# Attention of a two-block model: the steps written out in one fixed order

## Chip, cores, metric

The kernel runs on one core of a Trainium2 chip. The metric is the device time of one execution in microseconds, as a median of runs.

## What is computed

The model is two blocks on 512 tokens of width 1024, all in float32. The first block has two layers with feed-forward parts and a pooling or convolution mixer. The second has a gated linear attention (GLA) and a softmax attention side by side, gates for both, a merge and a feed-forward part. The change is in the softmax attention of the second block:

```python
qx = apply_rope(rms_norm_2(split_heads(aq, N_Q_HEADS, HEAD_DIM), q_norm), cos, sin)   # 8 heads of 128
kx = apply_rope(rms_norm_2(split_heads(ak, N_KV_HEADS, HEAD_DIM), k_norm), cos, sin)  # 2 heads, 512 tokens
kc = rms_norm_2(split_heads(ak_c, N_KV_HEADS, HEAD_DIM), k_norm)                      # 256 context tokens
s = jnp.einsum('bqhgd,bkhd->bhgqk', q_blk, k) * (HEAD_DIM ** -0.5)                    # k: 512 + 256 rows
p = jax.nn.softmax(s, axis=-1)
o = jnp.einsum('bhgqk,bkhd->bqhgd', p, v)
```

The merge then takes sigmoid(gate_a) * (attn @ w_br_attn) + sigmoid(gate_g) * (gla @ w_br_gla). The 16 gate projections (8 row tiles for each of the two gates) don't depend on the attention.

## The kernel before

Everything is kept transposed: a tile has 128 channels as partitions and 512 tokens as columns. Each float32 operand is split in a high and a low part of the type fp32r (`split`, L181: ScalarE casts the high part, VectorE subtracts it for the low part), and each product is three matmuls (`mm3`, L191: low weight, high weight, and high weight with the low part of the moving operand). A projection (`proj`, L197) is eight such products over 512 columns: 24 matmuls. Weights come by DMA from SyncE's queue into three raw buffers and are split into two buffers for high and two for low parts (`weights` of block 2, L578; `chunk`, L172).

The program's text is not the order in which the engines run. A scheduler with a timeline of its own orders each engine's instructions ahead of time by their place in the text and by when their inputs are ready in that timeline. On the chip each engine then takes them in that order. `keep_in_program_order` (L188) holds an instruction at its place. In the GLA phase just ahead, `run` (L697) goes through a list of steps and pins the first matmul of each step; the GLA steps and half projections (`halves`, L749; `gate_steps`, L797) alternate there. The last six steps of that phase already include gate projections.

The attention phase (L1009) has no pins but in small helpers. Its text: query 0; the two key heads, each for the 256 context and the 512 own tokens (squares, token sums on TensorE, a power on GpSimd in `rstd`, the sums spread by TensorE, the rotation `rotate` L1106, and a split); the values of six token tiles; and then for each of eight heads the query of the next head (L1060), a gate projection (L1066), and two halves of 256 query rows. A half has two tiles of scores (L1078 to L1080, 6 matmuls of 384 columns each), the softmax (L1081 to L1086), 12 transposes of the probabilities in three groups (L1094), the split of each group into PTh and PTl, and 18 matmuls for the product with values (L1099). There are two probability buffers (`probs`). PSUM has one pj bank for projections, one po bank, two tp banks and two sc buffers of two banks (L587). The query's token sums take the pj bank (L1023). `merge_gates(3)` (L1103) makes the last three gates. Each gate is stored to DRAM and read back by the merge.

The rope table (L1014) is loaded into memory that the last gate of the GLA phase used, so its DMA waits for that gate's DMA.

Of the kernel before, what the change touches and what calls it, by code (L numbers as in the profile page):

```python
# [9 lines left out]
F32 = mybir.dt.float32  # L10
# [21 lines left out]
GH = 4  # L32
# [116 lines left out]
class Builder:  # L149
# [35 lines left out]
    def pin(self, ins):  # L185

        if self.mark:
            self.tc.keep_in_program_order(ins)  # L188
            self.mark = False

    def mm3(self, ps, whi, wlo, xhi, xlo, start, stop):  # L191
        mm = self.nc.tensor.matmul
        self.pin(mm(ps, wlo, xhi, start=start, stop=False))  # L193
        mm(ps, whi, xhi, start=False, stop=False)  # L194
        mm(ps, whi, xlo, start=False, stop=stop)  # L195
# [501 lines left out]
    def run(self, steps):  # L697

        for step in steps:
            self.mark = True  # L700
            step()
        self.mark = False
# [83 lines left out]

    def merge_gates(self, n):
        for i in range(self.ngates, min(self.ngates + n, 2 * KT)):
            w = self.wm(self.gate_at(i))
            ps = self.psum("pj")  # L790
            self.proj(ps, w, self.hs)
            sg = self.ptmp.tile([P, T], F32, name="sg", tag="sq")
            self.sigmoid(sg, ps)
            self.nc.scalar.dma_start(self.gsave[i], sg)
            self.ngates = i + 1
# [180 lines left out]
    def value_rows(self, ps, wv, tt, ks, per, width):  # L976
        for k in ks:
# [6 lines left out]
            self.pin(mm(o, xl[:, t0:t0 + P], hi[:, s], start=(k == 0), stop=False))  # L984
            mm(o, xh[:, t0:t0 + P], hi[:, s], start=False, stop=False)  # L985
            mm(o, xh[:, t0:t0 + P], lo[:, s], start=False, stop=(k == KT - 1))  # L986
# [22 lines left out]
    def attention_phase(self, ctx):  # L1009
# [7 lines left out]
        def query(hd):  # L1017
            w = self.wm(WM_AQ + hd)
            ps = self.psum("pj")
            self.proj(ps, w, self.hs)  # L1020
            sq = self.ptmp.tile([P, T], F32, name="qsq", tag="sq")
            nc.scalar.activation(sq, ps, AF.Square)
            sums = self.psum("pj", "qsum")  # L1023
            self.token_sums(sums, sq, 4)
            r = self.rstd(sums[:, 0:4], 4, P, "q")
            rs = self.psmall.tile([P, 4], F32, name="rs4")
            nc.vector.tensor_scalar(rs, r[:, 0:4], QSCALE, None, ALU.mult)
            qf = p2.tile([P, T], F32, name="qf", tag="qf")
            nc.scalar.activation(qf, ps, AF.Copy, scale=self.vec("q_norm_2", 0, 1))
            qr = self.rotate(p2, qf)  # L1030
# [26 lines left out]
        for hd in range(8):  # L1057
            kv = hd // 4
            qh, ql, rs = nxt
            if hd < 7:  # L1060
                nxt = query(hd + 1)
# [185 lines left out]
```

## Time and profile before

| | |
|---|---|
| median of 3 runs | 2756.4 us (2752.97 to 2758.74) |
| the profiled execution | 2755.51 us, its span 2753.7 us |
| TensorE busy | 2701.2 us, 98% of the span |
| VectorE, ScalarE busy | 56%, 35% of the span |
| mean granted clock of TensorE | 0.997 |
| attention phase, first query projection to first branch product | 2032.2 to 2265.3 us |

A wait is time in which an engine stands still before an instruction; the profile names what ended it. A busy TensorE is not yet one at full speed: the granted clock of a stretch says which share of 2.4 GHz it had, and 0.5 is 1.2 GHz.

### The profile page before, as it was taken

The numbers are of one execution on the slowest core, as the hardware profiler recorded it, in microseconds if no ns is written. First come the engines' busy times: TensorE is split into PE (matmuls) and PEld (weight loads), VectorE is DVE, ScalarE is ACT, GpSimd is POOL, SyncE is SP. The second block draws the span as 40 slices with busy tenths as digits, with TensorE's granted clock in tenths as the row PEclk, the third lists the DMA queues.
The fourth block names the chain that finished last, engine by engine and source line by source line (L and its number), as shares of the span: only waits on it lengthen the run. The fifth ranks groups of instructions, "written<-read, shape, count | busy, mean of one in ns | idle before, by whom it ended". The sixth has DMA issues, their size and how long they took to land.

```text
span 2753.7 us, 34613 instructions
## 1 busy us (share of the span) xinstructions
PE 2701.2 (98%) x14005; PEld 2329.1 (85%) x14005; DVE 1532.4 (56%) x2499; ACT 950.6 (35%) x1474; POOL 36.0 (1%) x47
## 2 busy tenths in 40 slices
PE   7999999999999999999999998999999999999999
PEld 6888889888898888888988888888888888988887
DVE  6645567444466455754774556555546665554433
ACT  4222244222242222322432234544356662333322
POOL 0000000000000000000000000000010000000000
PEclk9999999999999999999999999999999999999999
DMA  8745543444536454433364542211111125333332
GB/s 316 253 140 189 184 146 122 147 133 135 166 116 209 140 173 156 128 101 99 118 213 142 169 139 78 73 54 47 58 62 62 58 78 183 96 100 94 98 99 78
DMA packets 102978, 354.42 MB, mean 129 GB/s; under 512 B 11425, under 2 KB 11681, under 8 KB 102689
## 3 DMA queue, kind: packets, MB, share of 16 engines
q1 hardware_dynamic: 100512, 348.00, 39.2%
q10 hardware_dynamic: 2304, 4.20, 0.4%
q8 instruction: 110, 1.80, 0.3%
q14 instruction: 52, 0.42, 0.0%
HBM read 343.76 MB, written 8.39 MB: 128 GB/s over the span
## 4 chain that ended last, share of the span: by engine, by line
PE 95%; DVE 2%; ACT 2%; DMA 1%; issue 0%; POOL 0%; SPq 0%; DVEq 0%; ACTq 0%
PE mm L193 29%; PE mm L194 28%; PE mm L195 28%; PE mm L984 1%; PE mm L986 1%; PE mm L985 1%; PE mm L904 1%; PE mm L991 1%; PE mm L1094 1%; ACT whi L182 1%; PE mm L446 0%; PE mm L492 0%; PE nR L273 0%; PE sc L1078 0%; DVE wlo L183 0%
## 5 line engine op out<-in xcount | busy, mean ns | idle before, releaser
L193 PE MATMUL mm<-hh,wlo 128*128 128x512 f32 (+1 forms) x2344 | 883.6, 379 | 2.8 <-ACT hh L289 1.8
L194 PE MATMUL mm<-hh,whi 128*128 128x512 f32 (+1 forms) x2344 | 878.2, 377 | 0.0
L195 PE MATMUL mm<-hl,whi 128*128 128x512 f32 (+1 forms) x2344 | 869.1, 377 | 0.4 <-DVE hl L290 0.3
L182 ACT CAST whi<-wraw 128x1024 fp32r<-128x1024 f32 (+1 forms) x443 | 456.8, 1034 | 907.1 <-PE mm L195 481.7
L183 DVE TENSOR_TENSOR wlo<-wraw,whi 128x1024 fp32r<-128x1024 f32 (+1 forms) x443 | 532.6, 1204 | 292.3 <-ACT whi L182 290.7
L193 PEld LDWEIGHTS mm<-hh,wlo 128*128 128x128 f32 x2344 | 442.4, 189 | 81.8 <-ACT hh L289 2.2
L194 PEld LDWEIGHTS mm<-hh,whi 128*128 128x128 f32 x2344 | 441.9, 189 | 77.5
L195 PEld LDWEIGHTS mm<-hl,whi 128*128 128x128 f32 x2344 | 437.0, 189 | 80.6 <-DVE hl L290 0.8
L194 PE MATMUL mm<-g,whi 128*128 128x512 f32 (+1 forms) x1147 | 416.1, 363 | 0.0
L193 PE MATMUL mm<-g,wlo 128*128 128x512 f32 (+1 forms) x1147 | 416.0, 363 | 0.0
L195 PE MATMUL mm<-g,whi 128*128 128x512 f32 (+1 forms) x1147 | 413.7, 362 | 0.0
L312 DVE SCALAR_TENSOR_TENSOR x<-mm,mod,x 128x512 f32<-128x512 f32 (+1 forms) x171 | 113.9, 666 | 319.9 <-PE mm L195 319.9
L194 PEld LDWEIGHTS mm<-g,whi 128*128 128x128 f32 x1147 | 216.5, 189 | 33.6
L193 PEld LDWEIGHTS mm<-g,wlo 128*128 128x128 f32 x1147 | 216.5, 189 | 33.5
L195 PEld LDWEIGHTS mm<-g,whi 128*128 128x128 f32 x1147 | 216.4, 189 | 33.4
L238 DVE SCALAR_TENSOR_TENSOR adaw<-adaw,cond 128x1024 f32<-128x1024 f32 x176 | 208.7, 1219 | 1.9 <-DMA adaw<-in_ada_dram 1.9
L351 DVE TENSOR_TENSOR gf<-sa,mm 128x512 f32<-128x512 f32 (+1 forms) x94 | 61.2, 652 | 201.3 <-PE mm L195 192.6
L350 ACT ACTIVATE sa<-mm 128x512 f32<-128x512 f32 (+1 forms) x94 | 53.6, 570 | 321.0 <-PE mm L195 321.0
L289 ACT ACTIVATE hh<-hn,mod 128x256 fp32r<-128x256 f32 (+1 forms) x120 | 57.9, 517 | 63.1 <-DVE hn L288 54.0
L257 DVE TENSOR_TENSOR nacc<-nacc,sq 128x256 f32<-128x256 f32 (+1 forms) x108 | 51.9, 485 | 29.5 <-ACT sq L256 28.7
L909 DVE TENSOR_TENSOR Z<-Z,tot 128x640 f32<-128x640 f32 x56 | 44.0, 827 | 39.5 <-PE mm L904 39.5
L256 ACT ACTIVATE sq<-x 128x256 f32<-128x256 f32 (+1 forms) x90 | 42.1, 468 | 66.2 <-DVE x L312 64.0
(271 smaller groups left out, 2580.7 us busy)
## 6 DMA issues: line engine op xcount, KB each, us to landing
wraw<-in_ffn_in_dram SPq DMA_DIRECT2D x176, 512.0 KB, 3.5
adaw<-in_ada_dram SPq DMA_DIRECT2D x176, 512.0 KB, 4.7
wraw<-in_wm_dram SPq DMA_DIRECT2D x66, 512.0 KB, 3.6
wraw<-in_mlp_dram SPq DMA_DIRECT2D x64, 512.0 KB, 3.7
wraw<-in_ffn_out_dram SPq DMA_DIRECT2D x64, 448.0 KB, 3.4
wraw<-in_ffn_out_dram SPq DMA_DIRECT2D x32, 512.0 KB, 3.6
wraw<-in_conv_in_dram SPq DMA_DIRECT2D x24, 512.0 KB, 3.5
ads<-in_ada_dram SPq DMA_DIRECT2D x8, 512.0 KB, 10.2
```

The source lines that it names most:

```text
L182: self.nc.scalar.copy(hi, src)
L183: return self.nc.vector.tensor_tensor(lo, src, hi.bitcast(F32), ALU.subtract)
L193: self.pin(mm(ps, wlo, xhi, start=start, stop=False))
L194: mm(ps, whi, xhi, start=False, stop=False)
L195: mm(ps, whi, xlo, start=False, stop=stop)
L238: nc.vector.scalar_tensor_tensor(out, raw, 1.0, self.cond[:, cond], ALU.mult, ALU.mult, accum_out=dst)
L257: nc.vector.tensor_tensor(acc, acc, sq[:, :n], ALU.add)
L289: nc.scalar.activation(hi, u, AF.Identity, bias=sh[:, k:k + 1])
L312: self.nc.vector.scalar_tensor_tensor(x, ps[:, :seg[1]], gate[:, k:k + 1], x, ALU.mult, ALU.add)
L350: nc.scalar.activation(sa, pa[:, :seg[1]], AF.Silu)
L351: nc.vector.tensor_tensor(gf, sa, pb[:, :seg[1]], ALU.mult)
L909: nc.vector.tensor_tensor(a, a, other.unsqueeze(2).to_broadcast([P, w // 2, s]), ALU.mult)
```

## The change

The attention phase becomes one list of steps, and in it every matmul and transpose is pinned (`run(..., True)` sets `strict`, in which `pin` keeps its mark). The opening alternates the two halves of query 0's projection with the key sums, the key norms and the values in parts. The key sums of a head share one tp bank and one power; the spread sums take an sc buffer each, and so do the values of token tiles 2 and 3. The query's sums move from the pj to a tp bank. Then come 16 steps, one for each half head: its scores, the product with values of the half before, the sums of the next query (in odd steps), the first half of a projection, two groups of transposes, the second half of the projection, and the third group. The projection is the next head's query in even steps, and a gate in odd ones and in step 14. The last gate stands between the last transposes and the last product with values. The number of matmuls, transposes, weight tiles and gates is the same.

The removed body of the attention phase stands above; it is cut here.

```diff
--- before.py
+++ after.py
@@ -186,13 +186,13 @@
 
         if self.mark:
             self.tc.keep_in_program_order(ins)
-            self.mark = False
+            self.mark = self.strict
 
     def mm3(self, ps, whi, wlo, xhi, xlo, start, stop):
         mm = self.nc.tensor.matmul
         self.pin(mm(ps, wlo, xhi, start=start, stop=False))
-        mm(ps, whi, xhi, start=False, stop=False)
-        mm(ps, whi, xlo, start=False, stop=stop)
+        self.pin(mm(ps, whi, xhi, start=False, stop=False))
+        self.pin(mm(ps, whi, xlo, start=False, stop=stop))
 
     def proj(self, ps, w, xs, seg=None):
         hi, lo = w
@@ -694,12 +694,13 @@
         self.run([tail[0], last[0], tail[1], last[1], tail[2], last[2], tail[3], last[3], tail[4], m[0], tail[5], m[1],
                   tail[6], m[2], tail[7], m[3], tail[8]])
 
-    def run(self, steps):
-
+    def run(self, steps, strict=False):
+
+        self.strict = strict
         for step in steps:
             self.mark = True
             step()
-        self.mark = False
+        self.mark = self.strict = False
 
     def gate_weights(self, cp):
 
@@ -783,16 +784,6 @@
-
-    def merge_gates(self, n):
...
@@ -973,7 +964,8 @@
             self.value_rows(ps, wv, tt, range(KT), per, width)
             evac(tt, ps[:, 0:width])
 
-    def value_rows(self, ps, wv, tt, ks, per, width):
+    def value_rows(self, ps, wv, tt, ks, per, width, which=(0, 1, 2)):
+
         for k in ks:
             xh, xl = (self.hs if tt < 4 else self.hcs)[k]
             t0 = (tt if tt < 4 else tt - 4) * P
@@ -981,9 +973,9 @@
             s = slice((k % per) * width, (k % per + 1) * width)
             mm = self.nc.tensor.matmul
             o = ps[:, 0:width]
-            self.pin(mm(o, xl[:, t0:t0 + P], hi[:, s], start=(k == 0), stop=False))
-            mm(o, xh[:, t0:t0 + P], hi[:, s], start=False, stop=False)
-            mm(o, xh[:, t0:t0 + P], lo[:, s], start=False, stop=(k == KT - 1))
+            for n in which:
+                self.pin(mm(o, (xl, xh, xh)[n][:, t0:t0 + P], (hi, hi, lo)[n][:, s], start=(k == 0 and n == 0),
+                            stop=(k == KT - 1 and n == 2)))
 
     def state_step(self, S, ktok, v, total):
         nc = self.nc
@@ -1015,92 +1007,146 @@
         K = [(cp.tile([P, T + C], F32R, name=f"Kh{i}"), cp.tile([P, T + C], F32R, name=f"Kl{i}")) for i in range(2)]
         Vh, Vl = cp.tile([P, 6, 256], F32R, name="Vh"), cp.tile([P, 6, 256], F32R, name="Vl")
         def query(hd):
...
+
+            Q = SimpleNamespace()
+
+            def end(ps):
+                Q.sq = self.ptmp.tile([P, T], F32, name="qsq", tag="sq")
+                nc.scalar.activation(Q.sq, ps, AF.Square)
+                qf = p2.tile([P, T], F32, name="qf", tag="qf")
+                nc.scalar.activation(qf, ps, AF.Copy, scale=self.vec("q_norm_2", 0, 1))
+                qr = self.rotate(p2, qf)
+                Q.h = p2.tile([P, T], F32R, name="qh", tag="qh")
+                Q.l = p2.tile([P, T], F32R, name="ql", tag="ql")
+                self.split(Q.h, Q.l, qr)
+
+            def sums():
+                ps = self.psum("tp", "qsum")
+                self.token_sums(ps, Q.sq, 4)
+                r = self.rstd(ps[:, 0:4], 4, P, "q")
+                Q.rs = self.psmall.tile([P, 4], F32, name="rs4")
+                nc.vector.tensor_scalar(Q.rs, r[:, 0:4], QSCALE, None, ALU.mult)
+
+            Q.steps = self.halves(lambda: (self.wm(WM_AQ + hd), self.psum("pj")), self.hs, end)
+            Q.sums = sums
+            return Q
+
+        parts = ((T, C, 0, 0), (0, T, 512, 2))
+        kr = {}
+
+        def key_sums(i):
+            ps = self.psum("tp", "ksum")
+            for at, n, _, col in parts:
                 sq = self.ptmp.tile([P, T], F32, name="ksq", tag="sq")[:, :n]
...
+                nc.scalar.activation(sq, self.kraw[i][:, at:at + n], AF.Square)
+                self.token_sums(ps, sq, n // P, col)
+            kr[i] = self.rstd(ps[:, 0:6], 6, P, "k")
+
+        def key_norm(i):
+            R = self.psum("sc", "kR", 1024)
+            for at, n, to, col in parts:
+                self.spread(R[:, to:to + n], kr[i], n // P, col)
+            for at, n, to, col in parts:
                 kf = p2.tile([P, T], F32, name="kf", tag="qf")
...
+                nc.scalar.activation(kf[:, :n], self.kraw[i][:, at:at + n], AF.Copy, scale=self.vec("k_norm_2", 0, 1))
                 if at == 0:
                     kf = self.rotate(p2, kf)
...
+                t = p2.tile([P, T], F32, name="kr", tag="kr", bufs=1)
+                nc.vector.tensor_tensor(t[:, :n], kf[:, :n], R[:, to:to + n], ALU.mult)
+                self.split(K[i][0][:, at:at + n], K[i][1][:, at:at + n], t[:, :n])
+
+        wv, vp = [], {}
+
+        def values(tts, half):
+            if not wv:
+                wv.extend(self.chunk(d["wv"][GH - 1, i]) for i in range(2))
+            if not half:
+                if tts[0] == 2:
+                    b = self.psum("sc", "sc", 1024)
+                    vp.update({2: b[:, 0:512], 3: b[:, 512:1024]})
+                else:
+                    vp.update({tts[0]: self.psum("pj"), tts[1]: self.psum("po")})
+                for tt in tts:
+                    self.value_rows(vp[tt], wv, tt, range(4), 4, 256)
+                return
+            for tt in tts:
+                self.value_rows(vp[tt], wv, tt, range(4, KT), 4, 256, (0, 1))
+            for tt in tts:
+                self.value_rows(vp[tt], wv, tt, range(4, KT), 4, 256, (2,))
+                self.split(Vh[:, tt], Vl[:, tt], vp[tt][:, 0:256])
+
+        attn, probs, PT = [], {}, {}
+
+        def scores(i, Q):
+            kv, half = i // 8, i % 2
+            probs[i] = []
+            for j in range(2):
+                qt = half * 2 + j
+                sl = slice(qt * P, (qt + 1) * P)
+                pr = p2.tile([P, 768], F32, name="probs", tag="probs", bufs=2)
+                mx = self.psmall.tile([P, 8], F32, name="mx")
+                sc = self.psum("sc", "sc", 1024).rearrange("p (e n) -> p e n", e=2)[:, :, 0:384]
+                for e in range(2):
+                    es = slice(e * 384, (e + 1) * 384)
+                    self.pin(nc.tensor.matmul(sc[:, e], Q.l[:, sl], K[kv][0][:, es], start=True, stop=False))
+                    self.pin(nc.tensor.matmul(sc[:, e], Q.h[:, sl], K[kv][0][:, es], start=False, stop=False))
+                    self.pin(nc.tensor.matmul(sc[:, e], Q.h[:, sl], K[kv][1][:, es], start=False, stop=True))
+                nc.vector.reduce_max(mx[:, 2:3], sc, AX.XY)
+                nc.vector.scalar_tensor_tensor(mx[:, 3:4], mx[:, 2:3], -1.0, Q.rs[:, qt:qt + 1], ALU.mult, ALU.mult)
+                nc.scalar.activation(pr.rearrange("p (e n) -> p e n", e=2), sc, AF.Exp, bias=mx[:, 3:4], scale=Q.rs[:, qt:qt + 1],
+                                     accum_out=mx[:, 6:7])
+                nc.vector.reciprocal(mx[:, 7:8], mx[:, 6:7])
+                nc.vector.tensor_scalar(pr, pr, mx[:, 7:8], None, ALU.mult)
+                probs[i].append(pr)
+
+        def turn(i, groups):
+            for g in groups:
+                hi = p2.tile([P, 2, 256], F32R, name=f"PTh{g}", tag=f"PTh{g}")
+                lo = p2.tile([P, 2, 256], F32R, name=f"PTl{g}", tag=f"PTl{g}")
+                PT[i, g] = hi, lo
+                ps = self.psum("tp")
+                for a in range(2):
+                    for j in range(2):
+                        kt = 2 * g + a
+                        o = a * 256 + j * P
+                        self.pin(nc.tensor.transpose(ps[:, o:o + P], probs[i][j][:, kt * P:(kt + 1) * P], self.ident))
+                self.split(hi.rearrange("p a q -> p (a q)"), lo.rearrange("p a q -> p (a q)"), ps)
+
+        def sum_values(i):
+            hd, half = divmod(i, 2)
+            if not half:
+                attn.append((self.pah.tile([P, T], F32R, name=f"ath{hd}", tag=f"ah{hd}"), self.pal.tile([P, T], F32R, name=f"atl{hd}")))
+            po = self.psum("po")[:, 0:256]
+            vs = slice((hd // 4) * P, (hd // 4 + 1) * P)
+            for kt in range(6):
+                hi, lo = PT[i, kt // 2]
+                self.mm3(po, Vh[:, kt, vs], Vl[:, kt, vs], hi[:, kt % 2], lo[:, kt % 2], kt == 0, kt == 5)
+            s = slice(half * 256, (half + 1) * 256)
+            self.split(attn[hd][0][:, s], attn[hd][1][:, s], po)
+
+        Q = query(0)
+        self.run([Q.steps[0], lambda: key_sums(0), Q.steps[1], lambda: key_sums(1), lambda: key_norm(0),
+                  lambda: values((0, 1), 0), Q.sums, lambda: values((0, 1), 1), lambda: key_norm(1),
+                  *(lambda a=a, n=n: values(a, n) for a in ((2, 3), (4, 5)) for n in range(2))], True)
+        sums = []
+        for i in range(16):
+            hd, half = divmod(i, 2)
+            if half == 0 and hd < 7:
+                N = query(hd + 1)
+                fill = N.steps
+            else:
+                N, fill = None, self.gate_steps()
+            work = [lambda: scores(i, Q)]
+            if i:
+                work.append(lambda: sum_values(i - 1))
+            self.run([*work, *sums, fill[0], lambda: turn(i, (0, 1)), fill[1], lambda: turn(i, (2,))], True)
+            sums = [N.sums] if N else []
+            if half == 0:
+                after = N
+            else:
+                Q = after
+        m = self.gate_steps()
+        self.run([*m, lambda: sum_values(15)], True)
         return attn
```

## Rows read from the trace of the kernel before

**Rows 1.** The page, busy time of the engines.

```profile
PE 2701.2 (98%) x14005; PEld 2329.1 (85%) x14005; DVE 1532.4 (56%) x2499; ACT 950.6 (35%) x1474; POOL 36.0 (1%) x47
```

**Rows 2.** Who TensorE waited for, 2032 to 2266 us: total, times, longest.

```profile
PE mm L193 <- ACT PTh L182: 4.9, 2, 3.3
PE sc L1078 <- ACT probs L1083: 2.7, 5, 0.5
PE mm L984 <- DVE qm L267: 1.4, 1, 1.4
PE mm L193 <- DVE qm L267: 1.0, 1, 1.0
PE mm L1094 <- DVE PTl L183: 0.2, 1, 0.2
```

**Rows 3.** Stretches of 2 us: length, busy PE PEld DVE ACT POOL, then PEclk.

```profile
2042.00:2044.00 2.00, 1.91 (x9) 1.91 (x10) 1.24 (x3) 1.95 (x5) 1.82 (x1) 0.55 0.00 0
...
2044.00:2046.00 2.00, 2.00 (x14) 2.00 (x13) 0.76 (x2) 0.85 (x2) 0.77 (x2) 0.59 0.73 225
...
2078.00:2080.00 2.00, 2.00 (x10) 1.64 (x9) 1.48 (x4) 0.57 (x1) 0.40 (x1) 1.00 0.46 188
...
2260.00:2262.00 2.00, 1.08 (x4) 0.85 (x5) 0.79 (x2) 2.00 (x5) 0.00 (x0) 0.67 0.00 0
...
2262.00:2264.00 2.00, 2.00 (x11) 2.00 (x10) 1.18 (x2) 0.99 (x2) 0.00 (x0) 0.50 0.35 130
```

**Rows 4.** One steady head, from score matmul to score matmul.

```profile
2134.31:2158.06 23.75, 23.22 (x140) 20.98 (x140) 16.54 (x33) 15.45 (x29) 1.01 (x1) 1.00 0.18 57
```

**Rows 5.** Timeline of ScalarE before the last product with values.

```profile
2257.46 2.92 ACT L182 CAST whi<-wraw 128x1024 fp32r<-128x1024 f32 x3
...
2260.28 0.58 ACT L182 CAST PTh<-mm 128x512 fp32r<-128x512 f32 x1
```

**Rows 6.** Timeline of TensorE, first and thirteenth matmul of a run of 512 columns.

```profile
2135.46 0.39 PE L193 MATMUL mm<-hh,wlo 128*128 128x512 f32 x1
...
2138.22 0.39 PE L193 MATMUL mm<-hh,wlo 128*128 128x512 f32 x1
```

**Rows 7.** The steady head from 2110.56 us, groups by line: busy us, mean ns.

```profile
L1083 ACT ACTIVATE probs<-sc,mx,rs 128x768 f32<-128x768 f32 x4 | 4.0, 1010 | 0.0
...
L183 DVE TENSOR_TENSOR PTl<-mm,PTh 128x512 fp32r<-128x512 f32 x6 | 4.0, 684 | 1.4 <-ACT PTh L182 1.4
...
L182 ACT CAST PTh<-mm 128x512 fp32r<-128x512 f32 x7 | 3.9, 591 | 1.2 <-PE mm L1094 1.2
...
L1081 DVE TENSOR_REDUCE mx<-sc 128x1 f32<-128x768 f32 x4 | 3.8, 951 | 2.6 <-PE sc L1080 2.6
...
L1086 DVE TENSOR_SCALAR probs<-probs,mx 128x768 f32<-128x768 f32 x4 | 2.5, 623 | 0.2
...
L1111 ACT COPY sw<-qf 32x512 f32<-32x512 f32 x4 | 2.5, 618 | 0.1
...
L182 ACT CAST whi<-wraw 128x1024 fp32r<-128x1024 f32 x2 | 2.1, 1054 | 0.0
...
L1083 ACT ACTIVATION_READ_ACCUMULATOR probs<-sc,mx,rs 128x1 f32 x4 | 0.9, 217 | 0.0
...
L1085 DVE RECIPROCAL mx<-mx 128x1 f32<-128x1 f32 x4 | 0.6, 158 | 0.5 <-ACT probs L1083 0.5
...
L1029 ACT ACTIVATE qf<-mm,vecs 128x512 f32<-128x512 f32 x1 | 0.7, 683 | 0.0
...
L1022 ACT ACTIVATE qsq<-mm 128x512 f32<-128x512 f32 x1 | 0.6, 597 | 1.1 <-PE mm L195 1.1
```

**Rows 8.** Timeline of VectorE in the opening.

```profile
2041.28 0.69 DVE L1113 TENSOR_TENSOR t<-qf,rope 128x512 f32<-128x512 f32 x1 [6.38 <-DMA rope<-in_rope_dram]
...
2053.32 0.69 DVE L1053 TENSOR_TENSOR kr<-t,kR 128x512 f32<-128x512 f32 x1
```

**Rows 9.** Timeline of TensorE in the stage ahead.

```profile
1855.92 0.39 PE L986 MATMUL mm<-wlo,hc 128*128 128x256 f32 x1 [2.42 <-DVE wlo L183]
```

More of the change, by code (lines that the diff above doesn't have):

```diff
@@ L785, in sigmoid @@
         act(out, out, AF.Exp, scale=-1.0)
-    def merge_gates(self, n):
[L788 to L795, printed above, removed]
     def gate_steps(self):
@@ L1017, in query @@
         def query(hd):
[L1018 to L1027, printed above, removed]
@@ L1028, in query @@
-            qf = p2.tile([P, T], F32, name="qf", tag="qf")
-            nc.scalar.activation(qf, ps, AF.Copy, scale=self.vec("q_norm_2", 0, 1))
-            qr = self.rotate(p2, qf)
-            qh = p2.tile([P, T], F32R, name="qh", tag="qh")
-            ql = p2.tile([P, T], F32R, name="ql", tag="ql")
-            self.split(qh, ql, qr)
-            return qh, ql, rs
-        attn = []
-        nxt = query(0)
-        for i in range(2):
-            for n, at in ((C, T), (T, 0)):
-                raw = self.kraw[i][:, at:at + n]
-                sq = self.ptmp.tile([P, T], F32, name="ksq", tag="sq")[:, :n]
-                nc.scalar.activation(sq, raw, AF.Square)
-                sums = self.psum("tp", "ksum")
-                self.token_sums(sums, sq, n // P)
-                r = self.rstd(sums[:, :n // P], n // P, P, "k")
-                R = self.psum("tp", "kR")
-                self.spread(R, r, n // P)
+            Q = SimpleNamespace()
@@ L1048, in attention_phase @@
                 kf = p2.tile([P, T], F32, name="kf", tag="qf")
-                nc.scalar.activation(kf[:, :n], raw, AF.Copy, scale=self.vec("k_norm_2", 0, 1))
+                nc.scalar.activation(kf[:, :n], self.kraw[i][:, at:at + n], AF.Copy, scale=self.vec("k_norm_2", 0, 1))
                 if at == 0:
                     kf = self.rotate(p2, kf)
-                kr = p2.tile([P, T], F32, name="kr", tag="kr", bufs=1)
-                nc.vector.tensor_tensor(kr[:, :n], kf[:, :n], R[:, :n], ALU.mult)
@@ L1103, in attention_phase @@
-        self.merge_gates(3)
+                t = p2.tile([P, T], F32, name="kr", tag="kr", bufs=1)
[19 more added lines that the diff above has]
+                self.split(Vh[:, tt], Vl[:, tt], vp[tt][:, 0:256])
@@ L1194, in setup @@
         self.mod = {}
-        self.mark = False
+        self.mark = self.strict = False
         self.pre = []
```

49 lines of the change are left out of this document (removed).

## Prediction, made before the run

> **What bounds the kernel now.** I read the page's busy shares first, then the waits of TensorE in the stage that the diff touches, then the clock around those waits, then one steady head of that stage by groups of instructions, and last the timelines of ScalarE and VectorE where TensorE waits longest.
>
> TensorE is busy for 98% of the span [rows 1]. The diff keeps every matmul, transpose and weight tile; it changes the order, some PSUM tags and where two small norms are computed. So it can win back only time in which TensorE stands still, or runs at the lower clock, between the first query projection (about 2032 us) and the first branch product of the merge (2265.3 us). TensorE's waits in that stage are five groups [rows 2]: 4.9 us in two waits for the high half of the transposed probabilities (the longer is 3.3 us, so the shorter about 1.6), 2.7 us in five waits of about 0.5 us for the exponential, 1.4 and 1.0 us for a VectorE instruction that reads the query's sums, and 0.2 us for a split. Together 10.2 us.
>
> Two waits cost more than their length, because the granted clock falls behind them. After the 1.4 us wait it is 0.55 and 0.59 in the two stretches of 2 us from 2042 us, after the 3.3 us wait 0.67 and 0.50 in the two from 2260 us: the level of 1.2 GHz instead of 2.4 for part or all of each stretch [rows 3]. Busy time times the missing share of the clock is 1.91 x 0.45 + 2.00 x 0.41 = 1.68 us for the first, and 1.08 x 0.33 + 2.00 x 0.50 = 1.36 us for the second. The head from 2134 us, with its 0.5 us wait, keeps clock 1.00 [rows 4]. So the stage holds 10.2 + 3.0 = 13.2 us to win: 0.48% of the span. That is the ceiling.
>
> **What the diff removes.** The 3.3 us wait at the end has a plain cause: ScalarE runs three casts of merge weights (2.92 us from 2257.46) ahead of the cast of the transposed probabilities that TensorE needs, which starts at 2260.28 [rows 5]. At that point TensorE has no other work left. In the new order the last gate's 24 matmuls stand between the last transposes and the last product with values. Twelve matmuls of 512 columns take 2138.22 - 2135.46 = 2.76 us [rows 6], so the cover is 5.5 us, more than those three casts and the split together (2.92 + 0.59 + 0.68, durations in [rows 5, 7]). I count the wait, and its slow clock, as gone: 3.3 + 1.36 = 4.7 us. If the cover failed it would all come back.
>
> The 1.4 us wait goes with the PSUM tag. Before, the query's sums sit in the single pj bank, and the value matmuls that want that bank wait for a VectorE read queued behind an instruction that waits for the rope table's DMA [rows 2, 8]. Now the sums use a tp bank, and the value matmuls follow the projection. The 1.0 us wait has the same cause one head later and goes in the same way. The five waits of 0.5 us come from a probability buffer: there are two, and the exponential that writes one waits for the last transpose that reads it, with a score matmul behind that exponential. In the new order all transposes of a half stand ahead of the next half's scores, so I count those 2.7 us, the 1.6 us wait (where ScalarE ran copies of the rotation ahead of the cast; what is left of it is priced below) and the 0.2 as gone too. Removed in all: the 13.2 us.
>
> **What it adds.** Every matmul of the stage now keeps the program's place, so a late operand stops everything behind it. Three places can do that.
>
> First, half 0, where there is no earlier half to work on. From the end of the first tile's scores: reduction 0.95, a one-column product like the reciprocal 0.16, exponential 1.01 and 0.22 for its sum; the second tile's exponential follows the first on ScalarE, another 1.23; then reciprocal 0.16 and scaling 0.62 [rows 7], 4.35 us in sum with no hand-off, about 4.65 with five or six of 0.05 us (my choice). The second tile's scores end 1.05 us later (six matmuls of 384 columns at three quarters of 0.23 us), so both probabilities are ready 3.6 us behind the last score. Only the first half of a projection, 2.76 us, stands there, less about 0.15 for the overlap of its start. The wait is 1.0 us, once. If the slow clock followed it, 1.5 more.
>
> Second, the steady halves. Here the previous half's product with values stands in between as well, 18 matmuls of 256 columns at about 0.12 us, 2.1 us, so the cover is 4.9 us (5.8 where the query's sums stand there too) against 3.6. The slack of 1.1 to 2.0 us is for ScalarE's queue. It is fullest behind a query projection: square 0.60, scaled copy 0.68, four copies of the rotation at 0.62 and the cast of the last transposed group 0.59 [rows 7], 4.35 us, some 4 us as such rows overlap by about 0.1 each. The first exponential is wanted 2.9 us after the projection's end (0.4 of transposes, 1.05 of scores, 1.1 for reduction and scale, and hand-offs), so it is some 1.1 us late. That the slack of 2.0 covers; a cast of the next weights, 1.05 us [rows 7], that comes in between leaves 0.2 us. Behind a gate projection ScalarE has less to do. The lower end is nothing. The upper end is that the cast of the last group stands behind the four copies: then its low half on VectorE comes 1.6 us after TensorE wants it. I take 0.3 us for each of seven heads, 2.1 us: nearer to the low end, because in the head shown ScalarE is busy 15.45 and VectorE 16.54 us of 23.75 [rows 4], and because in such a queue the wait of a copy for its own input is filled by the next ready cast.
>
> Third, the opening. Both key norms and the values of token tiles 2 and 3 share the two sc buffers, so those values wait until the first key head's rotated part has been multiplied by its norm. Counted from the query projection's start, TensorE comes to them after the projection (5.5), the values of tiles 0 and 1 (48 matmuls of 256 columns, 5.8), and four sets of 12 small key matmuls and one of 8 for the query (some 6.1 at 0.11 each): 17.4 us. The multiply's own chain, by [rows 7, 8]: the query's square and copy from 6.8 to 8.1 us; a key copy and the four rotation copies to 11.1; two VectorE instructions of 0.69 and a cast of 0.62 to 13.2; the key's four copies to 15.7; three of 0.69 to 17.8, with hand-offs 18. In the trace before, the multiply ends 21.8 us behind that start (2053.32 + 0.69 - 2032.2) [rows 8], because VectorE stood behind the norm's sums, which now come first; the rope table's landing at 9.1 us is not the last of its inputs. The squares of the second key head share two buffers with the query's square and can be late too. Lower end nothing; upper end the old 21.8 us, a wait of 4.4. I take 1.5: 0.6 for this chain and 0.9 for whatever else VectorE does in it.
>
> Added: 1.0 + 2.1 + 1.5 = 4.6 us. **The sum:** 13.2 - 4.6 = 8.6 us less. The profiled execution took 2755.5 us (span 2753.7), which gives 2746.9; the median of the runs shown is 0.9 us above that execution, so I forecast 2747.8 us.
>
> As a check from another side: the stage just ahead already runs its steps in a written order, and its waits there are mostly a value matmul waiting 2.42 us for the low half of a weight, once per head [rows 9]. A fixed order costs where a weight is late; in the new loop each weight has a whole half (11 us) to be split in.
>
> **The rivals.** *ScalarE's queue sets the pace in each head*: the casts of the last transposed group stand behind the rotation's copies, 1.6 us in each of seven heads, 11.2 us in place of 2.1. Gain 13.2 - 1.0 - 11.2 - 1.5 = -0.5: 2756.9 us, no change. For it: the queue keeps its order whatever is ready, as the three casts of [rows 5] show. Against: the casts are ready before the copies end.
>
> *The opening waits*: the sc buffer comes free only at the old time, 4.4 us late, and the clock falls behind it as it did after the 1.4 us wait, 1.5 more: 5.9 in place of 1.5. Gain 4.2: 2752.2 us, within the bound.
>
> *Slower, by the clock*: the wait in each head is long enough that the clock falls behind it as well, 1.6 + 1.5 = 3.1 us in seven heads, 21.7. Then 13.2 - 1.0 - 1.5 - 21.7 = -11 us: 2767 us. It is slower by more than 0.2% from (10.7 + 5.5) / 7 = 2.3 us a head on. Against it: the 0.5 us waits kept clock 1.00 [rows 4], and so did the 1.6 us wait, with 1.00 in the 2 us from 2078 behind it [rows 3]. The Trainium skill, "TensorE: Matmul & The Clock Gate", in "A second HAM failure mode: psum-queue depth-cycling", tells of a kernel whose short idles between groups of matmuls made the clock go down and up again and again; by that rule every head here would pay, and the time would be this rival's 2767 us. The trace shows the fall behind two waits (1.4 and 3.3 us) and none behind the 1.6 us wait or the five short ones.
>
> **How the numbers follow.** About 0.2% (5.5 us) is what a measurement of this kernel can tell from no change; the three runs shown span 5.8 us. Forecast 0.58 (own range 2743 to 2751), ScalarE's queue 0.20, the opening 0.13, slower by the clock 0.09. Faster 0.58, same 0.33, slower 0.09. The low end is the ceiling of 13.2 us less a microsecond of spread, 2742; the high end takes in the first two rivals, 2757.5.
>
> **What would show it.** In the profile after: the wait before the last product with values gone and the clock 1.00 to the stage's end; no wait of TensorE for the query sums' reader; no wait of score matmuls for the exponential; one wait of about 1 us at the first transposes; the steady head at 23.0 to 23.3 us instead of 23.75. Wrong would be waits of transposes for the scaled probabilities, or of value products for the low half of the transposed ones, in every head, or a wait of several us at the values of tiles 2 and 3.

## The result and the profile after

The change made the kernel slower: 2802.5 us against 2755.0 (medians of four runs each), a ratio of 1.0167 with a 95% interval of 1.0149 to 1.0185. Forecast were 2747.8 us, within 2742.0 to 2757.5.

The profiled execution after has a span of 2796.4 us, 42.7 more than before. Query 0 starts at 2032.2 us in both traces, and the first branch product of the merge at 2305.88 instead of 2265.30, so 40.6 us of the 42.7 lie in the stage that the diff touches. Right behind that mark the clock is 0.50, 0.50 and 0.62 in the three stretches of 2 us from 2306, where the kernel before keeps 1.00 behind its mark: 2.00 x 0.50 + 2.00 x 0.50 + 2.00 x 0.38 = 2.8 us, which is of the size of the other 2.1. The page of the kernel after, busy time, against [rows 1]:

```profile
PE 2718.8 (97%) x14005; PEld 2339.0 (84%) x14005; DVE 1533.7 (55%) x2497; ACT 952.4 (34%) x1474; POOL 37.4 (1%) x45
```

As many matmuls as before, but 17.6 us more of busy time for them: part of them ran at the lower clock. Who TensorE waited for, 2020 to 2320 us of the kernel after (total, times, longest), against [rows 2]:

```profile
PE mm L193 <- DVE wlo L183: 13.2, 1, 13.2
PE mm L195 <- DVE PTl L183: 8.8, 7, 1.3
PE ksum L261 <- ACT ksq L1041: 5.5, 2, 3.9
PE mm L1112 <- DVE probs L1099: 4.9, 9, 0.7
PE mm L1112 <- ACT probs L1096: 1.2, 1, 1.2
PE sc L977 <- DVE Vl L183: 0.9, 1, 0.9
PE mm L193 <- ACT sg L784: 0.2, 1, 0.2
```

All five groups of [rows 2] are gone, as forecast, and 34.7 us of new waits stand in their place, where 10.2 stood. One steady head, from one wait at the transposes to the next, and stretches of 2 us inside the following head (columns as in [rows 3]), against the 23.75 us of [rows 4]:

```profile
2105.97:2133.16 27.19, 25.32 (x140) 22.06 (x141) 16.42 (x32) 15.58 (x28) 1.48 (x1) 0.94 0.15 49
```

```profile
2140.00:2142.00 2.00, 1.08 (x10) 0.87 (x8) 2.00 (x3) 1.97 (x4) 0.00 (x0) 1.00 0.12 18
2142.00:2144.00 2.00, 1.67 (x13) 1.67 (x14) 1.84 (x8) 1.60 (x5) 0.00 (x0) 1.00 0.65 244
2144.00:2146.00 2.00, 2.00 (x7) 1.53 (x6) 1.89 (x7) 1.27 (x3) 1.48 (x1) 0.57 0.00 0
2146.00:2148.00 2.00, 2.00 (x7) 1.56 (x6) 0.48 (x1) 0.00 (x0) 0.00 (x0) 0.58 0.00 0
```

The granted clock falls to 0.57 and 0.58 behind the wait: of the two levels, 1.2 GHz instead of 2.4 for most of 4 us, which costs 2.00 x 0.43 + 2.00 x 0.42 = 1.7 us. It does not do so in every head. Of the seven waits of this kind, five have such a fall behind them; behind the first and the last, of the same length, the clock stays at 1.00:

```profile
2251.03 0.39 PE L195 MATMUL mm<-PTl,Vh 128*128 128x256 f32 x1 [1.27 <-DVE PTl L183]
```

```profile
2252.00:2254.00 2.00, 2.00 (x12) 1.76 (x13) 1.81 (x7) 1.97 (x6) 1.10 (x1) 1.00 0.13 53
2254.00:2256.00 2.00, 2.00 (x15) 1.72 (x14) 1.10 (x3) 0.14 (x1) 0.38 (x1) 1.00 0.00 0
```

The head of that last wait takes 25.55 us from score matmul to score matmul, the one ahead of it, with the fall, 27.16. In the first head the clock had already fallen, to 0.86, 0.50 and 0.79 from 2078 to 2084, behind the waits of 1.2 and 0.7 us at the first transposes. Now what stands around that wait, first on TensorE, then on ScalarE, then on VectorE:

```profile
2133.16 0.96 PE L1112 MATMUL mm<-ident,probs 128*128 128x128 f32 x7 [0.53 <-DVE probs L1099]
2142.33 0.39 PE L195 MATMUL mm<-PTl,Vh 128*128 128x256 f32 x1 [1.25 <-DVE PTl L183]
2160.35 0.95 PE L1112 MATMUL mm<-ident,probs 128*128 128x128 f32 x7 [0.51 <-DVE probs L1099]
```

```profile
2137.97 1.05 ACT L182 CAST whi<-wraw 128x1024 fp32r<-128x1024 f32 x1
2138.92 0.59 ACT L182 CAST PTh<-mm 128x512 fp32r<-128x512 f32 x1
```

```profile
2138.73 0.95 DVE L1094 TENSOR_REDUCE mx<-sc 128x1 f32<-128x768 f32 x1
2139.60 1.22 DVE L183 TENSOR_TENSOR wlo<-wraw,whi 128x1024 fp32r<-128x1024 f32 x1
2140.73 0.95 DVE L1094 TENSOR_REDUCE mx<-sc 128x1 f32<-128x768 f32 x1
2141.60 0.68 DVE L183 TENSOR_TENSOR PTl<-mm,PTh 128x512 fp32r<-128x512 f32 x1
```

The third group's cast (PTh) ends at 2139.51, but its low part (PTl) starts at 2141.60: VectorE first takes the low part of the weights (wlo) for the next half's projection, which TensorE comes to only at 2156.8, and a second reduction (the maximum of a tile of scores). The weights have two slots for each part, so one comes free when a projection ends, and the order laid down ahead of time puts the next split there. The Trainium skill, "PSUM — Partial Sum Buffer", section "Engine vs sequencer instructions", says that the queues of ScalarE and VectorE are strictly first in, first out; the trace agrees, with 2.1 us from the end of that cast to the start of the low part.

The end of the stage in the kernel after: TensorE, ScalarE, VectorE.

```profile
2305.88 0.77 PE L193 MATMUL mm<-ath,wlo 128*128 128x512 f32 x1 [13.21 <-DVE wlo L183]
```

```profile
2290.16 2.93 ACT L182 CAST whi<-wraw 128x1024 fp32r<-128x1024 f32 x3
```

```profile
2293.91 0.42 DVE L183 TENSOR_TENSOR atl<-mm,ath 128x256 fp32r<-128x256 f32 x1 [8.86 <-ACT ath L182]
2294.43 1.90 DVE L183 TENSOR_TENSOR gll<-gla,glh 128x512 fp32r<-128x512 f32 x3
2296.24 2.72 DVE L1173 SCALAR_TENSOR_TENSOR x<-x,vecs,fR 128x512 f32<-128x512 f32 x4
...
2303.86 0.74 DVE L1173 SCALAR_TENSOR_TENSOR x<-x,vecs,fR 128x512 f32<-128x512 f32 x1
2304.52 3.49 DVE L183 TENSOR_TENSOR wlo<-wraw,whi 128x1024 fp32r<-128x1024 f32 x3
```

The three high parts that [rows 5] show ahead of TensorE's cast are no hindrance any more. But their low parts stand on VectorE behind the eight splits of the GLA outputs (gll) and eight updates of the residual (x), 10.1 us from 2294.43, while VectorE idles 8.86 us before them. The first branch product waits 13.2 us. The opening is the third place: around and behind its two waits for the squares of the second key head (1.6 and 3.9 us) the clock is 0.50 in each stretch of 2 us from 2042 to 2052, such as the first. The second wait ends with the square in the last of these rows of ScalarE:

```profile
2042.00:2044.00 2.00, 0.00 (x0) 0.00 (x0) 1.23 (x1) 1.95 (x4) 0.00 (x0) 0.50 0.00 0
```

```profile
2041.45 1.04 ACT L182 CAST whi<-wraw 128x1024 fp32r<-128x1024 f32 x1
2042.51 2.50 ACT L1157 COPY sw<-qf 32x512 f32<-32x512 f32 x4
2045.03 0.63 ACT L1041 ACTIVATE ksq<-kraw 128x512 f32<-128x512 f32 x1
```

Here too an instruction that TensorE waits for stands behind others: a cast of weights and the four copies of the query's rotation.

### The profile page after: what moved, and what is told of

Same layout as the page of the kernel before. It is cut to its first block, busy times and chain, and to the rows that moved or that the text cites. A ratio compares the mean times of both kernels' runs of the same rounds, so it can differ in the third digit from the quotient of the medians.

```text
span 2796.4 us, 34599 instructions
## 1 busy us (share of the span) xinstructions
PE 2718.8 (97%) x14005; PEld 2339.0 (84%) x14005; DVE 1533.7 (55%) x2497; ACT 952.4 (34%) x1474; POOL 37.4 (1%) x45
## 4 chain that ended last, share of the span: by engine, by line
PE 93%; DVE 4%; ACT 2%; issue 1%; DMA 0%; POOL 0%; SPq 0%; ACTq 0%; DVEq 0%
PE mm L195 28%; PE mm L193 28%; PE mm L194 28%; PE mm L977 3%; DVE wlo L183 1%; PE mm L895 1%; PE mm L1112 1%; PE mm L983 1%; ACT probs L1096 1%; DVE mx L1094 1%; PE nR L273 0%; PE mm L446 0%; PE mm L492 0%; PE mm L479 0%; PE nsum L261 0%
## 6 DMA issues: line engine op xcount, KB each, us to landing
ads<-in_ada_dram SPq DMA_DIRECT2D x8, 512.0 KB, 10.1
```

## The experiments

The profiled executions differ ahead of the stage already, by some 5 us to either side, so each trace is also read by the stage itself: from its first key sums (twelve small matmuls; 2035.15 in the kernel after) to its first branch product (2305.88), 270.7 us. All ratios are to the kernel before; 0.001 is 2.75 us.

```
                              ratio   95% interval      median us   stage us
after                         1.0167  1.0149 to 1.0185  2802.5      270.7
e1_first_pins                 1.0117  1.0100 to 1.0133  2785.2
e2_weights_late               1.0057  1.0042 to 1.0072  2768.6      241.7
e4_keys_later                 1.0141  1.0122 to 1.0159  2790.9      265.8
e7_merge_weights_first        1.0117  1.0097 to 1.0137  2785.5      256.5
e6_sums_first                 1.0107  1.0089 to 1.0125  2783.3      256.9
e8_low_part_late              1.0047  1.0031 to 1.0063  2769.7      244.3
c1_all                        0.9983  0.9973 to 0.9994  2749.7      222.4
c2_all_loose                  0.9974  0.9964 to 0.9984  2747.6
c3_opening_loose              0.9974  0.9963 to 0.9984  2747.3
c4_loads_first                0.9977  0.9964 to 0.9990  2750.4
c5_residual_late              0.9956  0.9943 to 0.9970  2743.1
```

Where pins in the opening are loose, the key sums move against the rest and the stage has no like mark; there it is counted from query 0, from where the kernel before takes 233.1 us and the kernel after 273.7.

**Pins or order.** One theory blames the order of the casts (A), its rival the holding of every matmul (B). Here only the first matmul of each step is held.

```diff
-        self.run([*work, *sums, fill[0], lambda: turn(i, (0, 1)), fill[1], lambda: turn(i, (2,))], True)
+        self.run([*work, *sums, fill[0], lambda: turn(i, (0, 1)), fill[1], lambda: turn(i, (2,))])
```

(and so in the opening and at the end). 

> Only the first matmul of each step is held to its place, as before the change; the steps, their order, the banks and everything else stay. Theory A (the lost time comes from the casts: the next weights' split stands ahead of the split that the next product waits for, on ScalarE and VectorE): the waits of the trace after for the third low part (8.8 us in 7), for the merge weights (13.2) and for the squares (5.5) are not caused by the pins, so they stay, and the time stays within 8 us of 2802 (2794 to 2810). Theory B (holding every matmul is what costs, since nothing can slip into a hole of a wait): the holes fill and the time falls below 2775, towards 2755.

Neither range holds the measured 2785 us. The largest waits of this kernel, 2020 to 2320 us:

```profile
PE mm L193 <- DVE wlo L183: 13.2, 1, 13.2
PE mm L195 <- DVE PTl L183: 8.8, 7, 1.3
...
PE mm L193 <- DVE Vl L183: 2.7, 1, 2.7
PE ksum L261 <- ACT ksq L1041: 2.6, 2, 1.6
```

The two large groups stay to the tenth of a microsecond, so the pins don't make them. From query 0 to the first branch product it takes 266.1 us, 7.6 less than the kernel after. In the opening the wait of 3.9 us is 0.97, and the first scores come 31.8 us behind query 0 instead of 39.5; but the first head then takes 30.25 us instead of 26.10, with a new wait of 2.7 us for the values' low part, so that 3.5 us are left of the gain. Nearly all the rest is the clock: of the six heads that follow, three keep 1.00 and take 25.5 us, and three take 27.1, where the kernel after has one and five. Nothing shows that the pins set which. Holding every matmul costs in the opening, but isn't the main cause.

**The next weights.** In `scores`, behind the two tiles' softmax, the split of the next weights is now asked for, and held behind the last exponential (`ex`) and the last scaling (`last`); `issue_after` holds what is traced in it behind the instruction named, in the order that is laid down. The projections then take their weights from `ahead`; those lines are left out here.

```diff
+            with self.tc.issue_after(ex.ins), self.tc.issue_after(last.ins):
+                ahead[i + 1] = self.wm(fills[i + 1])
...
```

> The split of the weights for the next half projection is traced behind the scores of a half, and held behind the last exponential on ScalarE and the last scaling on VectorE, so that it can't stand ahead of the third transposed group's split. Theory A: the 8.8 us of waits for the third low part go, most of the 6.1 us of waits at the transposes too, and with them the half clock behind them, some 1.7 us in each of 7 heads (12 us): 21 to 27 us less, 2775 to 2782, and a head at 23.7 to 24.4 us where it took 27.2. Rival C (VectorE has too much to do in that stretch of a half, whatever the order): the wait moves to the weights' low part at the next half projection and the time stays within 6 us of 2802.

It went as theory A has it: the ratio falls by 0.0110, 30 us, the stage by 29.0. Rows of this kernel: a head, and the waits at the transposes.

```profile
2104.36:2127.38 23.02, 23.02 (x143) 20.85 (x142) 16.57 (x32) 15.65 (x29) 1.01 (x1) 1.00 0.17 58
```

```profile
PE mm L1114 <- ACT whi L182: 0.7, 1, 0.7
PE mm L1114 <- ACT probs L1096: 0.5, 1, 0.5
```

A head takes 23.02 us in which TensorE is busy all the time at full clock; the waits for the third low part are gone and those at the transposes fall from 6.1 to 1.2 us, all in half 0. Those at the end and in the opening are as in the kernel after. The gain is above the range given, and a head is shorter than the 23.7 to 24.4 us expected: 4.2 us (27.19 - 23.02) are won in it.

Which engine makes the low part late? The same edit with the hold on VectorE alone:

```diff
-            with self.tc.issue_after(ex.ins), self.tc.issue_after(last.ins):
+            with self.tc.issue_after(last.ins):
```

> Only the low part of the next weights, on VectorE, is held behind the last scaling of the half; the high part, on ScalarE, may stand ahead of the third transposed group's cast, as it does after the change. It tells which of the two engines makes the third low part late. If VectorE's 1.22 us do: the seven waits for the third low part go to 0 to 0.3 us each and the time is 2765 to 2772, as with both held. If ScalarE's 1.05 us do: the waits keep some 1 us each and the time is above 2790. If both do in a row: the waits halve, and with the half clock behind the shorter ones 2775 to 2788.

It is VectorE. ScalarE's and VectorE's timelines of this kernel behind a query projection:

```profile
2128.32 1.05 ACT L182 CAST whi<-wraw 128x1024 fp32r<-128x1024 f32 x1
2129.26 0.59 ACT L182 CAST PTh<-mm 128x512 fp32r<-128x512 f32 x1
```

```profile
2129.08 1.81 DVE L1094 TENSOR_REDUCE mx<-sc 128x1 f32<-128x768 f32 x2
2130.81 0.68 DVE L183 TENSOR_TENSOR PTl<-mm,PTh 128x512 fp32r<-128x512 f32 x1
```

The high part is still ahead of PTh on ScalarE, and both reductions are ahead of PTl; only the weights' low part has left VectorE. No wait for PTl is listed any more, and the time can't be told from that of the fuller edit (the intervals overlap). The trace shows a small rest: a head takes 23.39 us here, 0.37 more than with both held, and the stage 2.6 us more; what ScalarE's part costs there is not traced to rows.

**What a wait costs.** The query's sums are moved ahead of the product with values, so that TensorE comes later to the third low part, with the same work:

```diff
-            work = [lambda: scores(i, Q)]
+            work = [lambda: scores(i, Q), *sums]
...
-            self.run([*work, *sums, fill[0], lambda: turn(i, (0, 1)), fill[1], lambda: turn(i, (2,))], True)
+            self.run([*work, fill[0], lambda: turn(i, (0, 1)), fill[1], lambda: turn(i, (2,))], True)
```

> The query's sums (four small matmuls) are put ahead of the product with values instead of behind it, in every second half: nothing else is changed, the next weights stay early. So TensorE reaches the third low part 0.5 to 0.9 us later, with the same work in all. If a wait costs its own length alone, the seven waits of 1.25 us shrink to 0.35 to 0.75 and 4 to 6 us are won: 2796 to 2799. If the half clock behind a wait (2.4 us a head by the head's 27.19 us and the waits in it) goes with the longer of the waits, 15 to 22 us are won: 2780 to 2788.

Two groups of waits of this kernel, and the stretches behind the wait of 0.38 us that ends at 2138.18:

```profile
PE mm L1112 <- DVE probs L1099: 4.8, 9, 0.7
PE mm L195 <- DVE PTl L183: 2.6, 7, 0.4
```

```profile
2140.00:2142.00 2.00, 2.00 (x12) 1.56 (x11) 1.97 (x5) 1.13 (x3) 0.00 (x0) 1.00 0.00 0
2142.00:2144.00 2.00, 2.00 (x13) 1.75 (x12) 1.28 (x3) 1.07 (x2) 0.00 (x0) 1.00 0.03 8
```

The seven waits shrink by 6.2 us, the stage by 13.8 and the ratio by 0.0060 (16.5 us): the clock stays at 1.00 behind all seven shorter waits, so more than twice the waits' cut is won. The half clock's part in the loss is shown by this, not only read off the rows: a head takes 24.75 us, 2.4 less than one with the fall and 0.8 less than the one without, which is about the wait's own cut of 0.87.

**The opening.** The second key head's sums come later, behind the query's:

```diff
-        self.run([Q.steps[0], lambda: key_sums(0), Q.steps[1], lambda: key_sums(1), lambda: key_norm(0),
-                  lambda: values((0, 1), 0), Q.sums, lambda: values((0, 1), 1), lambda: key_norm(1),
+        self.run([Q.steps[0], lambda: key_sums(0), Q.steps[1], lambda: key_norm(0),
+                  lambda: values((0, 1), 0), Q.sums, lambda: key_sums(1), lambda: values((0, 1), 1), lambda: key_norm(1),
```

> In the opening the sums of squares of the second key head are put behind the query's sums, so that their squares find a free buffer; nothing else is changed. Theory A: the two waits for the squares (1.6 and 3.9 us) and the half clock behind them (about 2 us) go: 6 to 8 us less, 2794 to 2797. Rival D (the opening waits for ScalarE as a whole, the rotation and the key's copies included): the wait comes back before the second key's spread or the first scores, and the time stays within 2 us of 2802.

The ratio falls by 0.0026 (7 us), with intervals that overlap, and the stage by 4.9; so do the first scores, 34.6 us behind query 0 instead of 39.5. The waits for the squares go from 5.5 to 1.4 us, while the one for the values' low part grows from 0.9 to 1.6, so a part of the gain meets the next wait. That the place of the key sums cost this is shown. That the two buffers did is not: in the kernel after the second square runs from 2045.03, though the query's square keeps its buffer until its sums at 2053.9, and the other buffer is free from 2041.8, when the four sums ahead end. ScalarE has no gap from there on; it stands behind the cast and the copies shown above. Whether the taken buffer put it there when the order was laid down, no run separates.

**The end.** The first two merge weights take the two slots of the attention stage and are asked for ahead of the last half projection; what follows on ScalarE and VectorE is held behind their split:

```diff
-        self.run([*m, lambda: sum_values(15)], True)
+        self.run([m[0]], True)
+        self.early = [self.wm(base + 1) for base in (WM_MA, WM_MG)]
+        self.after = self.cast.ins, self.rest.ins
+        with self.tc.issue_after(self.after[0]), self.tc.issue_after(self.after[1]):
+            self.run([m[1], lambda: sum_values(15)], True)
...
```

(`cast` and `rest` are the two instructions of the last `split`; the GLA splits and the residual updates are held in the same way.) 

> The first two merge weights (attention's and GLA's) take the two slots of the attention stage, and their high and low parts are held ahead of the last half of the sixteenth gate's sigmoid, of the GLA splits and of the residual updates; nothing else is changed. Theory A (the 13.2 us at the stage's end are the low part of these weights standing behind 16 other VectorE instructions of 10.2 us): the wait falls to 0 to 2 us, and the half clock behind it goes: 12 to 16 us less, 2786 to 2790. Rival E (VectorE's work of the stage's end has to be done anyway before the GLA branch): the wait comes back as one for the low parts of the GLA outputs after 24 matmuls, and 3 to 7 us are won, 2795 to 2799.

It went as theory A has it: the ratio falls by 0.0050 (14 us), the stage by 14.2. The wait of 13.2 us is gone. A smaller one comes 14 us later, at the third merge weight:

```profile
2310.54 0.50 PE L194 MATMUL mm<-ath,wlo 128*128 128x512 f32 x1 [2.11 <-DVE wlo L183]
```

**Together.** The three edits e2, e4 and e7 in one kernel; then that with only the first matmul of each step held, everywhere or in the opening alone. 

> The three edits together: the next weights' split behind the scores, the second key head's sums behind the query's, the first merge weights ahead of the GLA splits. Theory A (three separate causes, each an order of casts on ScalarE and VectorE): the three gains of the stage add up, 29.0 + 4.9 + 14.2 = 48 us from the start of the stage's key sums to its first branch product, so the stage is some 7 us shorter than before the change and the time is 2740 to 2750, faster than before. Rival F (they share a cause, so that one gain contains another): 2755 to 2765, not faster than before.

> The three edits together, and only the first matmul of each step held to its place. Theory A: once the casts are in time there is no hole for a matmul to slip into in the steady halves, and the opening gains what it gained alone beyond the moved squares, some 4 us: 0 to 5 us below the three edits with every matmul held. Theory B (holding every matmul costs in the heads too): 8 us or more below them.

> The three edits together, and only in the opening is the first matmul of each step alone held to its place; the heads and the end hold every matmul. If the pins cost in the opening alone, this equals the version with loose pins everywhere within 2 us; if loose pins disorder the heads (with the next weights early they gave heads of 25.5 and 27.1 us in turn), it is faster than that one by 3 us or more.

The gains add up: 29.0 + 4.9 + 14.2 = 48.1 us expected, 270.7 - 222.4 = 48.3 measured in the stage. From query 0 on it takes 3.0 us more, 225.4, against 233.1 before: 7.7 us less. The ratio, 0.9983, gains only 4.7 us; the new wait at the third merge weight, 2.2 us, lies behind the mark and is most of the difference. Loose pins give 0.9974 in both forms, with intervals that overlap that of the held one. Their traces tell more: from query 0 to the first branch product both take some 3 us less than the held one, 222.3 and 222.4, and in all three each head behind the first takes 23.02 us. So the pins cost some 3 us in the opening, and neither "costs in the heads" nor "disorders the heads" shows; the heads of 25.5 and 27.1 us seen with loose pins before are told apart by the clock.

**The third merge weight.** On top of the three edits with a loose opening, its load (and the fourth's) is traced ahead of the residual's loads; then, in a second kernel, the residual updates and the first merge products are held behind its low part as well. Both steps in one diff, shortened:

```diff
+        self.early.append(self.wm(WM_MA + 3))
+        later = self.rest.ins
+        self.early.append(self.wm(WM_MG + 3))
...
-            with self.tc.issue_after(self.after[1]):
+            with self.tc.issue_after(later):
                 nc.vector.scalar_tensor_tensor(self.x[k], self.x[k], self.vec("final_g", k, 1), R1, ALU.mult, ALU.mult)
```

> The version with three edits and a loose opening, and the loads of the third and fourth merge weights traced ahead of the loads of the residual, so that on SP's queue seven of its eight loads no longer stand ahead of them. The 2.1 us wait for the third merge weight's low part (at 2267.83 in that version) should go: 2 to 4 us less, 2743 to 2746. If the low part is late for another reason, VectorE's 16 instructions ahead of it, nothing is won: 2746 to 2749.

> As the version before it, and the eight residual updates and the first merge products on VectorE are held behind the low part of the third merge weight. If VectorE's order makes that low part late, its wait of 2.8 us at the third merge product goes and the ratio to the kernel before falls by 0.001, to 0.9960 to 0.9972. If the wait passes to the fourth weight's low part, one merge product later, the ratio stays within 0.0005 of 0.9977.

The earlier load alone won nothing. VectorE's timeline of that kernel (c4) shows why:

```profile
2267.82 2.72 DVE L1190 SCALAR_TENSOR_TENSOR x<-x,vecs,fR 128x512 f32<-128x512 f32 x4 [0.25 <-DMA x<-xsave]
2270.51 0.69 DVE L1215 TENSOR_TENSOR my<-msg,mm 128x512 f32<-128x512 f32 x1
2271.19 0.69 DVE L1217 TENSOR_TENSOR msg<-msg,mm 128x512 f32<-128x512 f32 x1
2271.80 1.22 DVE L183 TENSOR_TENSOR wlo<-wraw,whi 128x1024 fp32r<-128x1024 f32 x1
```

With those held back too, the waits of the last kernel (c5) from 2020 to 2350 us are these three:

```profile
PE mm L194 <- DVE Vl L183: 1.0, 1, 1.0
PE ksum L262 <- ACT ksq L1042: 0.6, 1, 0.6
PE mm L194 <- ACT sg L785: 0.2, 1, 0.2
```

It is the fastest kernel of the study: 0.9956, 0.9943 to 0.9970, so 0.44% faster than before. Its interval overlaps the one of the kernel without these holds, and the ratio lies a little below the range given; that the wait is gone is shown, the size of what it gave is not.

## Why the prediction was wrong

**What the diff removes** was right: every group of [rows 2] is gone, and so is the end wait's cause in [rows 5]. Once the instructions that stood in the way in the three places were moved, the stage was 7.7 us shorter; 8.6 had been forecast. The head of 23.0 to 23.3 us that was to show it came out at 23.02.

**"I take 0.3 us for each of seven heads"** is the first step that failed. Only ScalarE's queue was summed there; the next weights' cast was seen (1.05 us, "leaves 0.2 us") but its other half, 1.22 us on VectorE, was not, nor that VectorE takes both of a half's reductions in the same stretch. e8 shows that it is VectorE's part alone that made the third low part late. The wait was 1.25 us, inside the bounds of 0 and 1.6, and the price was that of the rival *Slower, by the clock*, whose 3.1 us a head were given a chance of 9%: measured were 4.2 (27.19 - 23.02) in each of five heads, of which 1.8 are listed waits, 1.7 half clock, and the remaining 0.7 are not traced to rows; in the last head, without the half clock, 2.5. Against that rival stood the 0.5 us waits and one of 1.6 us that kept clock 1.00 [rows 3, 4]; they proved no measure for the 1.25 us wait. The granted clock falls and rises again behind that wait in five of the seven heads, to 0.57 in the head shown, and stays behind the other two. The rule of the Trainium skill that the prediction weighed there, "TensorE: Matmul & The Clock Gate", section "A second HAM failure mode: psum-queue depth-cycling", tells of short idles between groups of matmuls that make the clock go down and up again. The trace agrees for these five heads.

**"In the new loop each weight has a whole half (11 us) to be split in"** had the danger the wrong way round. In the heads no wait for a weight is listed; the weight was early, and what it stood ahead of was late.

**"I count the wait, and its slow clock, as gone"** for the end failed by another wait in its place. The cover of 5.5 us, the work that TensorE still has while the other engines finish, was reckoned against ScalarE's three casts and one split. What the first merge product needs next, its weight's low part on VectorE, and what stands ahead of that, was not asked: 13.2 us, in no bound and no rival. e7 shows it.

**"The squares of the second key head share two buffers with the query's square and can be late too"** named the squares and gave them no price, and what made the longer of their waits is ScalarE's order. The 1.5 us taken were for another wait, that of the values of tiles 2 and 3 for the sc buffer. It did not come: the first key head's multiply ended at 2053.04, and TensorE came to those values at 2058.91 without a wait. The 0.9 us there lie later, between tile 2's split and the last matmuls of tile 3 in the same buffer. The squares cost 5.5 us of waits and the half clock around and behind them for 10 us, and the opening's first score came 7.3 us later than before. Half 0's wait at the transposes was sized at 1.0 and measured 1.9 (1.2 and 0.7), and the slow clock, named there as 1.5 us more and not taken, did follow.

Together, over the stage before: 7.3 us in the opening, and 33.3 from the first scores to the first branch product. Of these, 13.2 at the end, less the 3.3 and 1.4 us that the old end wait had cost, make 8.5. The seven heads take 187.5 us (2071.68 to 2259.20); at the 23.75 us of a steady head before they would take 166.25, which gives an estimate of 21.3 more in them. The remaining 3.5 us are not traced to rows.

## What to carry to other kernels

Where an order is laid down ahead of time, a change of the matmuls' order also moves every cast that a freed buffer releases: list for each engine the instructions that become ready in the same stretch, and ask which of them nobody needs yet. Sum both halves of a two-engine operation; the half on the other engine is the one that gets forgotten. At the end of a stage, ask what the first product of the next stage needs and what stands ahead of it, not only whether the last wait of the old one is covered.

## What the runs showed of the hardware

A wait's length alone did not tell whether the clock falls. Behind seven waits of some 1.25 us in the kernel after, with the same matmuls around them, it fell in five heads (to 0.57 and 0.58 in the one shown) and stayed at 1.00 in two. Behind 0.38 us (e6) and 0.5 us it stayed at 1.00, and behind a wait of about 1.6 us in the kernel before it stayed at 1.00 too [rows 3]. No run here tells what decides. What a fall costs can be read from two heads of one kernel, with the same waits: 27.16 us with it, 25.55 without.

Single executions also fall apart ahead of the stage, by some 5 us to either side: the first key sums come at 2035.15 us in the kernel after, at 2039.95 with the merge weights moved and at 2030.28 with the three edits, though no edit changes the work ahead of them. The kernel before itself spans 2749.4 to 2761.4 us in 29 runs. The cause stays open.
